# Convolution taps in PSUM, gate products on GpSimd: one change to the up-projections of a two-layer trunk

## The chip, the core and the metric

The kernel runs on one core of a Trainium2 chip. The core has five engines: TensorE (PE) multiplies matrices and writes its sums to PSUM, VectorE (DVE) and ScalarE (ACT) work on elements and reach both SBUF and PSUM, GpSimd (POOL) works on elements in SBUF, and SyncE (SP) issues DMA transfers. The metric is the device time of one execution in microseconds (us); lower is better.

## What is computed

The reference is a trunk of two decoder layers in fp32, with 512 tokens and a model width of 1024. Each layer has a mixer, a gated MLP with a short convolution, and an embedding that is gated in. The change lies in the MLP:

```
D_MODEL, SEQ, D_FF, FFN_CONV_K = 1024, 512, 2816, 3

def _conv_ffn(h, w_up, conv_w, conv_b, w_down):
    u = _causal_depthwise_conv(h @ w_up, conv_w) + conv_b
    gate, up = jnp.split(u, 2, axis=-1)
    return (jax.nn.gelu(gate, approximate=False) * up) @ w_down

for i in range(2):
    x = x + mixer_i(rms_norm(x, mix_norm[i]))
    x = x + _conv_ffn(rms_norm(x, ffn_norm[i]), w_up[i], conv_w[i], conv_b[i], w_down[i])
    x = x + sigmoid(rms_norm(x, ple_norm[i]) @ ple_w_gate[i]) * (p[i] @ ple_w_proj[i])
```

The convolution runs over tokens: each of the 5632 columns of `h @ w_up` is multiplied by its own three weights at lags 0, 1 and 2, and added up with a bias. The RMS factor of each token, called `R` below, is not applied to `h`; the kernel multiplies the projected columns by it, ahead of the taps.

## The kernel before

**Layout.** Activations stand with features on the 128 partitions and the 512 tokens along the free axis. A projected column block is thus a tile of 128 x 512, one PSUM bank.

**Precision.** Every fp32 product is made of three faster ones: both operands are split into a high and a low part, and `mm3` (lines 165 to 171) issues high x high, high x low, low x high. Weights arrive by DMA as `raw` tiles and are split on the chip: ScalarE rounds to the high part `wh` (line 149, or line 825 in `cut_blocks`) and VectorE subtracts to get the low part `wl` (lines 150 and 826). TensorE's third product waits for `wl`.

**Groups.** The up-projection works in 11 groups per layer. A group has four column blocks: two of the value half, made by `value` with `mm3`, and two of the gate half. The gate blocks are computed by a scheme with seven products of half-size blocks instead of eight (`seven`, products at lines 878 to 880), for which VectorE forms differences of weight blocks: two in `first_forms` (lines 849 and 850) and two in `more_forms` (line 857, whose result is cut as `t2`, and line 860, whose result enters the cut called `last` in `seven`). The gate blocks come out in the PSUM banks X and Y, the value blocks in V1 and in a bank that was begun ahead of the group (the late column). Y lacks one term, which is copied to SBUF as `more` and added by VectorE at line 930. All of a group's products are matmuls of 128 x 128 by 128 x 256: 180 of them.

**After the products.** `taps` handles one column block: VectorE multiplies by `R` into an SBUF tile `z` (line 927; for Y it adds `more` at line 930 and multiplies at line 934), ScalarE multiplies `z` by the lag-0 weight and adds the bias, into one half of a tile pair `zt` (line 935), and VectorE adds the two lagged terms (line 937, on 511 and 510 tokens). A group has two such pairs, `g` for the gate and `y` for the value, from a ring of two buffers; `z` comes from a ring of three. `close` then applies Gelu to `g` on ScalarE (line 1087), and `place` multiplies gate and value on VectorE: two products of 128 x 512 for the first four groups of a layer (line 992), one of 128 x 1024 for the others (line 1002). From the fifth group on, `split_one` cuts the product of four groups earlier for the down-projection (lines 108 and 109).

**Order.** TensorE's order is written by hand (`manual_schedule`); each group issues the late column of the next group between its own V1 and its last products. VectorE, ScalarE, GpSimd and the SP queue get their order from a scheduler in the program's builder, with a few written constraints (`issue_after`). An engine runs its instructions in that order, and waits on semaphores for what other engines make.

**Elsewhere.** The pair buffers are used again in the down-projection, where weights are loaded straight into them (`load_inner`), and in layer 1 as halves for its last steps (`half`). There, in `ple1`, the output tiles come from the `z` ring (`result`, line 1423), and one more tile is kept in it.

Of the kernel before, what the change touches and what calls it, by code (L numbers as in the profile page):

```python
# [10 lines left out]
F32 = mybir.dt.float32  # L11
# [3 lines left out]
AF = mybir.ActivationFunctionType  # L15
ALU = mybir.AluOpType
# [3 lines left out]
P = 128  # L20
S = 512
# [42 lines left out]
class Kernel:  # L64
# [763 lines left out]
        n = 2 if wide else 1  # L828
        return lambda j, c: (h[:, n * j + c, :], l[:, n * j + c, :])

    def seven_forms(self, ev, od, raw=None):


        plain = self.first_forms(ev, od, raw)
        return plain, self.cut_blocks(ev), self.more_forms(ev, od)

    def first_forms(self, ev, od, raw=None):

# [11 lines left out]
        nc.vector.tensor_tensor(b12, b22, b12, ALU.subtract)  # L850
        return plain

    def more_forms(self, ev, od):

        nc = self.nc
        b11, b21, b22 = ev[:, :, :P], od[:, :, :P], od[:, :, P:]
        nc.vector.tensor_tensor(b11, b22, b11, ALU.subtract)
        with self.tc.high_priority(offset=40):
            t2 = self.cut_blocks(b11, False)
        nc.vector.tensor_tensor(b21, b21, b11, ALU.subtract)  # L860
        return t2

    def seven(self, od, ws, xg, forms, keep=True):
# [43 lines left out]
    def ffn(self, i, project, next_gain):  # L907


        nc, a, tc = self.nc, self.a, self.tc  # L910
        gain = self.g_ffn[i]
        wu = a["ffn_w_up"][i].rearrange("(k p) n -> p k n", p=P)
        w0, w1, w2, bb = self.fcv

        mine, other = (("a0", "a1"), ("b0", "b1"))[:: 1 - 2 * i]
        with tc.tile_pool(name=f"ffn{i}", bufs=1) as fp:
            self.mlp = fp
            kept, acts, fours = [None] * NF, [None] * NF, []
            groups = NF // 2

            def both():
                return fp.tile([P, 2, S], F32, tag="zt", name=self.nm("zt"), bufs=2)

            def taps(y, ps, f, more=None, behind=None):
                z = fp.tile([P, S], F32, tag="z", name=self.nm("z"), bufs=3)
                if more is None:
                    nc.vector.tensor_tensor(z, ps, R, ALU.mult)  # L927
                else:
                    h2 = lambda x: x.rearrange("p (u t) -> p u t", u=2)
                    nc.vector.tensor_tensor(  # L930
                        h2(z), h2(ps), more.unsqueeze(1).to_broadcast([P, 2, S // 2]), ALU.add
                    )
                    with tc.issue_after(behind.ins) if behind else nullcontext():
                        nc.vector.tensor_tensor(z, z, R, ALU.mult)
                nc.scalar.activation(y, z, AF.Identity, scale=w2[:, f : f + 1], bias=bb[:, f : f + 1])  # L935
                for tap, w in ((1, w1), (2, w0)):
                    nc.vector.scalar_tensor_tensor(  # L937
                        out=y[:, tap:], in0=z[:, : S - tap], scalar=w[:, f : f + 1], in1=y[:, tap:],
                        op0=ALU.mult, op1=ALU.add,
                    )  # L940

# [22 lines left out]
            def prepare(d, behind=None):  # L964

                if d == 0:
                    values.append(load_values(-1))
                rv = values.pop()
                with tc.issue_after(behind.ins) if behind else nullcontext():
                    w0 = column(rv, rv.shape[2] // P - 1)  # L970
                rg = self.raw(ND, 256)
                nc.sync.dma_start(rg, wu[:, :, 256 * d : 256 * d + 256])
                ev, od = self.by_parity(rg)
                ws = self.seven_forms(ev, od, rg)
                values.append(load_values(d))
                return self.seven(od, ws, xg, self.forms), w0, column(values[0], 0)

# [8 lines left out]
            def place(d, g, y):  # L986

                f = 2 * d
                if f < 8:
                    kept[f : f + 2] = [self.fp.tile([P, S], F32, tag=other[0], name=self.nm("u")) for _ in range(2)]  # L990
                    for u in range(2):
                        nc.vector.tensor_tensor(kept[f + u], g[:, u], y[:, u], ALU.mult)
                    return
                if d == groups - 1:
                    x = y
                else:
                    if f % 4 == 0:
                        fours.append(self.four(fp, F32))
                    x = fours[-1][:, f % 4 : f % 4 + 2]
                kept[f : f + 2] = [x[:, 0], x[:, 1]]  # L1000
                pairs[f] = x
                nc.vector.tensor_tensor(x, g, y, ALU.mult)

            pairs = {}

# [49 lines left out]
            with tc.manual_schedule(engines={ET.PE}):  # L1055
                late = begin(0, steps, w0c)
                close = lambda: None
                for d in range(groups):
                    g, y = both(), both()
# [9 lines left out]
                    if d == 0:  # L1069
                        R = self.spread()  # L1070
                    X, Y, more = next(steps)
# [280 lines left out]
    def ple1(self, fp):  # L1352
# [3 lines left out]
        nc, a, tc = self.nc, self.a, self.tc  # L1356
# [63 lines left out]
                self.mm3(pj, sl(pT[k], t), (w[0][:, k, :], w[1][:, k, :]), start=k == 0, stop=k == 1)  # L1420
            return pj

        def result():
            return fp.tile([P, S], F32, tag="z", name=self.nm("so"), bufs=3)

        def keep(banks, tag):
            out = []
# [33 lines left out]
        with tc.manual_schedule(engines={ET.PE, ET.DVE, ET.Activation}):  # L1461
            add(X, "e1", w11, first=True)
            wt1.append(chunk(b11[:, 2:, :]))
            minus(b11, b22, b11)
            steps = [(j, i, both, Q[i]) for j in range(J) for i in range(2)]
            add(None, "s1", wt1, first=True, order=steps[:2])

            sq = self.by_token()
            ka = [self.sp.tile([P, S], F32, tag=g, name=self.nm("keep"), bufs=n) for g, n in (("acc", 1), ("sq", 2))]
            for k, x in zip(ka, X):  # L1470
                nc.scalar.copy(k, x)
            wt2 = chunks(b11)
            pT = self.load_p(1, fp, pin)
            sums = self.few(NT, "ss")
            for t in range(NT):
                junk = self.sp.tile([P, P], F32, tag="vrow", name=self.nm("junk"))
                nc.scalar.activation(junk, sq[:, t * P : (t + 1) * P], AF.Copy, accum_out=sums[:, t : t + 1])
            self.end_norm(sums)
            add(None, "s1", wt1, order=steps[2:])
            minus(b12, b22, b12)  # L1480
            kd = keep(Q, "R")
            wt3 = chunks(b12)
            wj = chunk(wj_raw[:, 2:, :])
            steps = [(j, i, both, X[i]) for j in range(J) for i in range(2)]
            add(None, "s2", wt2, order=steps[:4])
            xs = [back(1, t) for t in (2, 3)]
            add(None, "s2", wt2, order=steps[4:])
            kb = [self.sp.tile([P, S], F32, tag="sq", name=self.nm("keep"), bufs=2), result()]
            for k, x in zip(kb, X):
                nc.scalar.copy(k, x)  # L1490
            pjs = [proj(t, wj) for t in (2, 3)]
            w22 = chunks(b22)
            minus(b11, b21, b11)
            wt4 = [chunk(b11[:, :2, :])]
            nc.scalar.activation(self.few(NT, "rs", 4), self.r, AF.Sigmoid)
            add(X, "s3", wt3)
            ss = [summed(X[t], kd[t]) for t in (0, 1)]
            for t in (0, 1):
                finish(1, t + 2, ss[t], xs[t], pjs[t], ss[t])
            steps = [(j, i, both, Q[i]) for j in range(J) for i in range(2)]  # L1500
            add(None, "s4", w22, order=steps[:6])
            xs = [back(1, t) for t in (0, 1)]
            pjs = [proj(t, wj) for t in (0, 1)]
            wt4.append(chunk(b11[:, 2:, :]))
            wj = chunk(wj_raw[:, :2, :])
            add(None, "s4", w22, order=steps[6:])
            ss = [summed(Q[t], kb[t]) for t in (0, 1)]

            halves = ((0, H // 2), (H // 2, H))
            Y = [Q[0]] + [y[:, : H // 2] for y in (Q[1], X[0])]  # L1510
            for t in (0, 1):
                finish(1, t, ss[t], xs[t], pjs[t], ss[t])
            nc.scalar.copy(Y[0], ka[0])
            nc.scalar.copy(Y[1], ka[1][:, : H // 2])
            steps = [(j, i, both, X[i]) for j in range(J) for i in range(2)]
            add(None, "o2", wt4, order=steps[:6])
            xs = [back(0, t) for t in (2, 3)]
            pjs = [proj(t, wj) for t in (2, 3)]
            w21 = chunks(b21)
            add(None, "o2", wt4, order=steps[6:])  # L1520
            for t in (0, 1):
                finish(0, t + 2, X[t], xs[t], pjs[t])
                if t == 0:
                    nc.scalar.copy(Y[2], ka[1][:, H // 2 :])
            add(None, "o1", w21, order=[(j, 0, both, Y[0]) for j in range(J)])
            xs = [back(0, t) for t in (0, 1)]
            pjs = [proj(t, wj) for t in (0, 1)]
            finish(0, 0, Y[0], xs[0], pjs[0])
            for y, c in zip(Y[1:], halves):
                add(None, "o1", w21, order=[(j, 1, c, y) for j in range(J)])  # L1530
                finish(0, 1, y, xs[1], pjs[1], None, *c)
# [471 lines left out]
```

## Time and profile before

| what | value |
|---|---|
| time of three runs | 1201.72, 1200.26 and 1200.0 us; median 1200.26 |
| span of the profiled execution | 1199.4 us (the median is 0.86 above it) |
| TensorE busy | 1192.4 us, 99% |
| VectorE busy | 966.4 us, 81% |
| ScalarE busy | 671.1 us, 56% |
| GpSimd busy | 44.8 us, 4% |
| nine groups of the up-projection, layer 0 and layer 1 | 184.00 and 184.51 us |

A row of a timeline has the start and the duration in us, the engine, the line of the kernel, the operation, the tile that is written and those that are read, partitions x elements, and a count. In brackets stands how long the engine had been idle, and which instruction ended that. A row of a source line has minimum, median and maximum duration in ns. A row of the view by windows has, for each engine, busy time and number of instructions in the stretch. Start-to-start distances are a little shorter than durations, because an engine's instructions overlap at their ends.

### The profile page before, as it was taken

Reading aid. Unit: us, or ns where it says so; the run is one execution under the profiler, and the core shown is the slowest. Engines: PE = TensorE matmul, PEld = TensorE weight load, DVE = VectorE, ACT = ScalarE, POOL = GpSimd, SP = SyncE. Lnnn points to the kernel's source line nnn. Section 1 sums busy time; section 2 is a strip of 40 time slices with the busy share of each in tenths; the row PEclk is TensorE's granted clock in tenths of the full one; section 3 lists DMA queues with packets and bytes.
Section 4 is the critical chain, followed back from the end, with each engine's and each line's share of the span. In section 5 each row is a group of like instructions: output and inputs, shape, how many; then the busy total and the mean of one; then the engine's idle time right before and its main releaser. Section 6 shows DMA issues by size and latency. Waiting matters only on the chain.

```text
span 1199.4 us, 19840 instructions
## 1 busy us (share of the span) xinstructions
PE 1192.4 (99%) x8074; PEld 1076.9 (90%) x8074; DVE 966.4 (81%) x1543; ACT 671.1 (56%) x1093; POOL 44.8 (4%) x64
## 2 busy tenths in 40 slices
PE   9999999999999999999999999999999999999998
PEld 8877789999999989888988988899999999888887
DVE  6786687898999986746679876687989999988595
ACT  7466565655565753534563655555555656655374
POOL 2610000000000000000100000000000000000000
PEclk9999999999999999999999999999999999999999
DMA  7232222333332342232322222223233333322601
GB/s 223 72 97 80 74 88 71 106 106 106 106 107 89 113 138 84 87 106 86 107 93 70 75 68 70 88 72 115 97 112 100 106 106 114 124 89 98 210 1 71
DMA packets 113216, 117.74 MB, mean 98 GB/s; under 512 B 2873, under 2 KB 108403, under 8 KB 113125
## 3 DMA queue, kind: packets, MB, share of 16 engines
q1 hardware_dynamic: 111760, 115.35, 29.5%
q8 instruction: 63, 1.03, 0.4%
q0 software_dynamic: 560, 0.42, 0.3%
q10 hardware_dynamic: 804, 0.70, 0.2%
q14 instruction: 29, 0.23, 0.1%
HBM read 114.37 MB, written 2.10 MB: 97 GB/s over the span
## 4 chain that ended last, share of the span: by engine, by line
PE 92%; DVE 5%; ACT 1%; DMA 1%; issue 0%; ACTq 0%; DVEq 0%
PE ps L169 14%; PE ps L170 14%; PE ps L171 14%; PE pa L170 7%; PE pa L171 7%; PE pa L169 7%; PE ps L878 5%; PE ps L880 5%; PE ps L879 5%; PE pa L878 2%; PE pa L880 2%; PE pa L879 2%; PE ps L1400 1%; PE ps L1398 1%; PE ps L1399 1%; DVE wl L150 1%
## 5 line engine op out<-in xcount | busy, mean ns | idle before, releaser
L149 ACT ACTIVATE wh<-raw 128x1024 fp32r<-128x1024 f32 (+4 forms) x154 | 152.5, 992 | 128.9 <-PE ps L170 92.8
L150 DVE TENSOR_TENSOR wl<-raw,wh 128x1024 fp32r<-128x1024 f32 (+4 forms) x154 | 175.3, 1140 | 57.9 <-ACT wh L149 57.0
L825 ACT ACTIVATE wh<-raw 128x1024 fp32r<-128x1024 f32 x78 | 83.0, 1064 | 115.8 <-DVE raw L850 75.9
L937 DVE SCALAR_TENSOR_TENSOR zt<-z,vfa,zt 128x510 f32<-128x510 f32 (+1 forms) x176 | 131.0, 745 | 0.3
L826 DVE TENSOR_TENSOR wl<-raw,wh 128x1024 fp32r<-128x1024 f32 x78 | 95.4, 1222 | 12.8 <-ACT wh L825 12.8
L171 PE MATMUL pa<-b,wl 128*128 128x256 f32 x352 | 97.3, 276 | 0.1
L171 PE MATMUL pa<-a,wl 128*128 128x256 f32 x352 | 97.2, 276 | 0.0
L169 PE MATMUL pa<-b,wh 128*128 128x256 f32 x352 | 97.2, 276 | 0.0
L169 PE MATMUL pa<-a,wh 128*128 128x256 f32 x352 | 97.2, 276 | 0.0
L170 PE MATMUL pa<-b,wh 128*128 128x256 f32 x352 | 97.2, 276 | 0.0
L170 PE MATMUL pa<-a,wh 128*128 128x256 f32 x352 | 97.2, 276 | 0.0
L935 ACT ACTIVATE zt<-z,vfb 128x512 f32<-128x512 f32 x88 | 71.5, 813 | 19.6 <-DVE z L927 9.5
L169 PE MATMUL ps<-b,wh 128*128 128x512 f32 x192 | 76.6, 399 | 0.0
L170 PE MATMUL ps<-b,wh 128*128 128x512 f32 x192 | 75.1, 391 | 0.0
L171 PE MATMUL ps<-b,wl 128*128 128x512 f32 x192 | 75.0, 391 | 0.0
L171 PEld LDWEIGHTS pa<-b,wl 128*128 128x128 f32 x352 | 66.1, 188 | 0.3 <-DVE wl L150 0.3
L169 PEld LDWEIGHTS pa<-b,wh 128*128 128x128 f32 x352 | 66.1, 188 | 0.0
L170 PEld LDWEIGHTS pa<-a,wh 128*128 128x128 f32 x352 | 66.1, 188 | 0.0
L169 PEld LDWEIGHTS pa<-a,wh 128*128 128x128 f32 x352 | 66.1, 188 | 0.0
L170 PEld LDWEIGHTS pa<-b,wh 128*128 128x128 f32 x352 | 66.1, 188 | 0.0
L171 PEld LDWEIGHTS pa<-a,wl 128*128 128x128 f32 x352 | 66.1, 188 | 0.0
L878 PE MATMUL ps<-four,wh 128*128 128x256 f32 x232 | 64.7, 279 | 0.0
(472 smaller groups left out, 3667.7 us busy)
## 6 DMA issues: line engine op xcount, KB each, us to landing
raw<-in_ffn_w_up_dram SPq DMA_DIRECT2D x42, 1024.0 KB, 5.1
raw<-in_ffn_w_down_dram SPq DMA_DIRECT2D x13, 1024.0 KB, 4.8
raw<-in_hy_w_in_dram SPq DMA_DIRECT2D x8, 1024.0 KB, 5.0
raw<-in_gla_w_in_dram SPq DMA_DIRECT2D x8, 1024.0 KB, 5.1
raw<-in_ffn_w_down_dram SPq DMA_DIRECT2D x8, 768.0 KB, 4.1
raw<-in_ple_w_gate_dram SPq DMA_DIRECT2D x6, 1024.0 KB, 4.6
raw<-in_hy_w_out_dram SPq DMA_DIRECT2D x16, 256.0 KB, 3.9
raw<-in_gla_w_out_dram SPq DMA_DIRECT2D x4, 1024.0 KB, 4.7
```

Of the source, the lines that this page charges most:

```text
L149: nc.scalar.activation(hv, v, AF.Copy)
L150: self.rest_cut = nc.vector.tensor_tensor(lv, v, hv.bitcast(F32), ALU.subtract)
L169: mm(out, lh, rh, start=start, stop=False, **kw)
L170: mm(out, lh, rl, start=False, stop=False, **kw)
L171: mm(out, ll, rh, start=False, stop=stop, **kw)
L825: nc.scalar.activation(h, src, AF.Copy)
L826: nc.vector.tensor_tensor(l, src, h.bitcast(F32), ALU.subtract)
L878: mm(out, wh, xh, start=first and j == 0, stop=False, **kw)
L879: mm(out, wh, xl, start=False, stop=False, **kw)
L880: mm(out, wl, xh, start=False, stop=j == ND // 2 - 1, **kw)
L935: nc.scalar.activation(y, z, AF.Identity, scale=w2[:, f : f + 1], bias=bb[:, f : f + 1])
L937: nc.vector.scalar_tensor_tensor(out=y[:, tap:], in0=z[:, : S - tap], scalar=w[:, f : f + 1], in1=y[:, tap:], op0=ALU.mult, op1=ALU.add,)
```

## The change

`taps` no longer has the tile `z`. VectorE multiplies by `R` in place, in the PSUM bank (for Y, it first adds `more` in place); ScalarE and the two lagged additions read that bank. Of the differences of weight blocks, the last one (`b21`) is made by GpSimd in the up-projections; `place` multiplies gate and value on GpSimd. The ring of pairs has three buffers instead of two. In `ple1` the output tiles come from the pairs, and the `z` ring has one buffer left, for the tile that is kept. The memory of both rings together is the same, 14 KB per partition.

```
-    def more_forms(self, ev, od):
+    def more_forms(self, ev, od, last=None):
...
-        nc.vector.tensor_tensor(b21, b21, b11, ALU.subtract)
+        (last or nc.vector).tensor_tensor(b21, b21, b11, ALU.subtract)
...
-                return fp.tile([P, 2, S], F32, tag="zt", name=self.nm("zt"), bufs=2)
+                return fp.tile([P, 2, S], F32, tag="zt", name=self.nm("zt"), bufs=3)

             def taps(y, ps, f, more=None, behind=None):
-                z = fp.tile([P, S], F32, tag="z", name=self.nm("z"), bufs=3)
-                if more is None:
-                    nc.vector.tensor_tensor(z, ps, R, ALU.mult)
-                else:
+                if more is not None:
                     h2 = lambda x: x.rearrange("p (u t) -> p u t", u=2)
                     nc.vector.tensor_tensor(
-                        h2(z), h2(ps), more.unsqueeze(1).to_broadcast([P, 2, S // 2]), ALU.add
+                        h2(ps), h2(ps), more.unsqueeze(1).to_broadcast([P, 2, S // 2]), ALU.add
                     )
-                    with tc.issue_after(behind.ins) if behind else nullcontext():
-                        nc.vector.tensor_tensor(z, z, R, ALU.mult)
-                nc.scalar.activation(y, z, AF.Identity, scale=w2[:, f : f + 1], bias=bb[:, f : f + 1])
+                with tc.issue_after(behind.ins) if behind else nullcontext():
+                    nc.vector.tensor_tensor(ps, ps, R, ALU.mult)
+                nc.scalar.activation(y, ps, AF.Identity, scale=w2[:, f : f + 1], bias=bb[:, f : f + 1])
                 for tap, w in ((1, w1), (2, w0)):
                     nc.vector.scalar_tensor_tensor(
-                        out=y[:, tap:], in0=z[:, : S - tap], scalar=w[:, f : f + 1], in1=y[:, tap:],
+                        out=y[:, tap:], in0=ps[:, : S - tap], scalar=w[:, f : f + 1], in1=y[:, tap:],
...
-                ws = self.seven_forms(ev, od, rg)
+                ws = self.seven_forms(ev, od, rg, nc.gpsimd)
...
-                        nc.vector.tensor_tensor(kept[f + u], g[:, u], y[:, u], ALU.mult)
+                        nc.gpsimd.tensor_tensor(kept[f + u], g[:, u], y[:, u], ALU.mult)
...
-                nc.vector.tensor_tensor(x, g, y, ALU.mult)
+                nc.gpsimd.tensor_tensor(x, g, y, ALU.mult)
...
-        def result():
-            return fp.tile([P, S], F32, tag="z", name=self.nm("so"), bufs=3)
+        result = self.half
...
-            kb = [self.sp.tile([P, S], F32, tag="sq", name=self.nm("keep"), bufs=2), result()]
+            kb = [
+                self.sp.tile([P, S], F32, tag="sq", name=self.nm("keep"), bufs=2),
+                fp.tile([P, S], F32, tag="z", name=self.nm("keep"), bufs=1),
+            ]
```

More of the change, by code (lines that the diff above doesn't have):

```diff
@@ L829, in cut_blocks, with seven_forms @@
         return lambda j, c: (h[:, n * j + c, :], l[:, n * j + c, :])
-    def seven_forms(self, ev, od, raw=None):
+    def seven_forms(self, ev, od, raw=None, last=None):
         plain = self.first_forms(ev, od, raw)
-        return plain, self.cut_blocks(ev), self.more_forms(ev, od)
+        return plain, self.cut_blocks(ev), self.more_forms(ev, od, last)
     def first_forms(self, ev, od, raw=None):
```

## The prediction

> **What bounds the kernel now.** I read the page of the profile first: engine totals and the chain that ended last.
>
> ```profile
> span 1199.4 us, 19840 instructions
> ...
> PE 1192.4 (99%) x8074; PEld 1076.9 (90%) x8074; DVE 966.4 (81%) x1543; ACT 671.1 (56%) x1093; POOL 44.8 (4%) x64
> ...
> PE 92%; DVE 5%; ACT 1%; DMA 1%; issue 0%; ACTq 0%; DVEq 0%
> ```
>
> TensorE sets the end: 99% busy, 92% of the chain. VectorE has 81% and 5% of the chain, so the change, which takes work off VectorE only, can win only where TensorE stands still for it. The view by windows, over nine groups of the up-projection in each layer:
>
> ```profile
> core 0: us, PE busy (x) PEld busy (x) DVE busy (x) ACT busy (x) POOL busy (x), PEclk, DMA share, GB/s
> 206.94:390.94 184.00, 184.00 (x1623) 183.90 (x1621) 170.08 (x228) 107.77 (x151) 0.00 (x0) 1.00 0.31 101
> 824.34:1008.85 184.51, 184.43 (x1622) 184.00 (x1621) 170.23 (x228) 107.41 (x151) 0.00 (x0) 1.00 0.31 101
> ```
>
> The granted clock is 1.00, and a group has 180 matmuls. Their pitch stands in TensorE's timeline.
>
> ```profile
> 302.76 0.28 PE L171 MATMUL pa<-a,wl 128*128 128x256 f32 x1
> ...
> 312.28 0.28 PE L880 MATMUL ps<-four,t 128*128 128x256 f32 x1
> ...
> 313.64 0.28 PE L171 MATMUL pa<-a,wl 128*128 128x256 f32 x1
> ```
>
> From 312.28 to 313.64 are twelve matmuls, 0.1133 us each. Nine groups without a stall are 9 x 180 x 0.1133 = 183.6 us: the first window loses 0.40, the second 0.91, together **1.31 us**. That is all that a faster VectorE can give back in these stages; the first group of each layer and the down-projections lie outside.
>
> How near is VectorE to being late? Its timeline, and ScalarE's beside it:
>
> ```profile
> 292.92 1.22 DVE L826 TENSOR_TENSOR wl<-raw,wh 128x1024 fp32r<-128x1024 f32 x1
> ...
> 297.27 1.23 DVE L1002 TENSOR_TENSOR four<-zt,zt 128x1024 f32<-128x1024 f32 x1 [1.19 <-ACT zt L1087]
> 298.72 1.23 DVE L150 TENSOR_TENSOR wl<-raw,wh 128x1024 fp32r<-128x1024 f32 x1 [0.22 <-ACT wh L149]
> ...
> 309.78 0.68 DVE L860 TENSOR_TENSOR raw<-raw 128x512 f32<-128x512 f32 x1
> 310.38 0.68 DVE L826 TENSOR_TENSOR t<-raw,t 128x512 fp32r<-128x512 f32 x1
> 310.98 0.68 DVE L927 TENSOR_TENSOR z<-pa,R 128x512 f32<-128x512 f32 x1
> 311.58 1.21 DVE L150 TENSOR_TENSOR wl<-raw,wh 128x1024 fp32r<-128x1024 f32 x1
> ```
>
> ```profile
> 291.79 1.07 ACT L825 ACTIVATE wh<-raw 128x1024 fp32r<-128x1024 f32 x1 [0.92 <-PE ps L879]
> ...
> 296.18 1.06 ACT L1087 ACTIVATE zt<-zt 128x1024 f32<-128x1024 f32 x1 [1.48 <-DVE zt L937]
> 297.35 0.36 ACT L902 COPY ps<-ps 128x256 f32<-128x256 f32 x1
> 297.62 1.06 ACT L149 ACTIVATE wh<-raw 128x1024 fp32r<-128x1024 f32 x1
> ```
>
> Low parts of weights reach TensorE with these leads: for V1, 311.58 + 1.21 = 312.79 against 313.64, **0.85 us**; for t2, 311.06 against 312.28, 1.22; for the late value column, 299.95 against 302.76, 2.81. VectorE's loop is tied to TensorE once per group: the cut of 292.92 starts when ScalarE's cut, released by TensorE, ends (291.79 + 1.07 = 292.86). VectorE then runs with two pauses, 1.19 for the Gelu and 0.22 for L149, until the next such cut. Any delay that it can't make good there is carried into the next group.
>
> **The change, part by part.** The built program keeps TensorE's order. VectorE loses 52 instructions, which GpSimd gains: 22 of L860 and 30 of the products at L992 and L1002.
>
> *L860 to GpSimd.* VectorE's chain between 298.72 and the V1 cut gets shorter by its pitch, 310.38 - 309.78 = **0.60 us**. Its result goes to the "last" cut, much later. On GpSimd it runs beside a tap and the addition, both with an operand in PSUM.
>
> *Gate times value to GpSimd.* VectorE no longer waits 1.19 for the Gelu nor multiplies (1.23). But its next operation, L150, still waits for ScalarE's L149, which ends at 297.62 + 1.06 = 298.68, so the cut of the late column starts no earlier; of this part nothing shortens the loop. Behind it, the split four groups later and the down-projection read the products; those are far off. The SP queue's loads into the pair buffers wait for the last product, but they are issued a down-projection stage ahead.
>
> What it can cost: GpSimd's product starts at the Gelu's end, 297.24, and runs through 298.72. GpSimd and VectorE beside each other, at the only place of this trace where both run:
>
> ```profile
> L518 POOL TENSOR_TENSOR m<-q,ropeS x8: 726/830/1182, 44.2 to 55.6; 128x256 f32<-128x256 f32 x8
> ```
>
> ```profile
> 44.24 3.26 POOL L518 TENSOR_TENSOR m<-q,ropeS 128x256 f32<-128x256 f32 x4 [9.21 <-ACT q L557]
> ...
> 49.58 1.04 POOL L738 TENSOR_TENSOR R<-R 128x512 f32<-128x512 f32 x1
> ...
> 54.88 1.62 POOL L518 TENSOR_TENSOR m<-q,ropeS 128x256 f32<-128x256 f32 x2 [0.39 <-DVE m L521]
> ```
>
> ```profile
> 45.67 1.25 DVE L516 TENSOR_TENSOR m<-q,ropeC 128x512 f32<-128x512 f32 x1
> ...
> 54.06 0.68 DVE L521 TENSOR_TENSOR m<-m,m 128x512 f32<-128x512 f32 x1
> ...
> 56.78 0.68 DVE L516 TENSOR_TENSOR m<-q,ropeC 128x512 f32<-128x512 f32 x1
> ```
>
> The same L516, two inputs in SBUF, takes 1.25 beside GpSimd and 0.68 without it: one waits for the other. L150 has two inputs in SBUF too, so I let it wait until the product is done. The hand-over to GpSimd is 54.88 - (54.06 + 0.68) = 0.14. No row shows 128x1024 on GpSimd. Call its time p. Low end: 1.04 and two more of the step from 256 to 512 elements, 1.04 + 2 x (1.04 - 0.726) = 1.67. High end: four of 0.726, 2.90. Twice the 512 row, the nearest, is 2.08. L150 is then late by 297.24 + 0.14 + p - 298.72 = p - 1.34; the 0.60 from L860 pays for that, so the loop keeps its pace up to **p = 1.94**. Above it the excess e = p - 1.94 is carried from group to group, and TensorE is late once ten groups of it pass the 0.85 lead: 10e - 0.85 per layer. At 1.67 the cost is 0; at 2.08, 2 x (1.4 - 0.85) = 1.1 us. I take the middle between these, **+0.5**, since even a small recovery of the blocked operation would bring 2.08 to 0; the ends are 0 and, at 2.90, 2 x (9.6 - 0.85) = 17.5.
>
> The Trainium skill, "GPSIMD Engine Reference", section 3.1 Elementwise, measures 4497 ns for 2048 fp32 elements in a tensor_tensor. An estimate from that page for half as many is 2.25 us; by it e would be 0.31 and the cost 2 x (3.1 - 0.85) = 4.5 us. No run here shows it.
>
> *Taps in PSUM.* Durations with the operand in PSUM and in SBUF, by source line:
>
> ```profile
> L112 DVE SCALAR_TENSOR_TENSOR a<-ps,vec,a x8: 741/744/752, 7.1 to 17.3; 128x512 fp32r<-128x512 f32 x8
> L112 DVE SCALAR_TENSOR_TENSOR a<-xT,vec,a x8: 745/747/750, 495.0 to 523.2; 128x512 fp32r<-128x512 f32 x8
> ```
>
> Reading PSUM is free (744 against 747 ns), so the eight taps of a group cost what they did. New is VectorE's writing to PSUM: four products with R and one addition per group. No row has it; ScalarE's copy within PSUM (L902, 0.36 for 256 columns) isn't slow. I take 0. Low end 0; as the high end I take 0.25 each, somewhat under half of the 1.25 - 0.68 = 0.57 by which L516 stretched when it shared its inputs: 1.25 a group, against the 0.60. A column's bank is held until its last tap instead of its first product. There are four of each kind, taken in turn, and the tap ends microseconds before the slot's next matmul: 0, hidden by the rotation; without that cover TensorE would wait for a tap, 0.74 a time.
>
> The Trainium skill, "VectorE: DVE Perf Modes", section "The TRN2 errata", charges 120 fixed cycles for a PSUM source and 58 for SBUF, some 65 ns more by its clock. The trace disagrees: 744 against 747 ns. If it held here, eight taps would add 0.52 a group.
>
> *Three pair buffers, one z buffer.* Same memory. The third pair lets the next taps start while GpSimd still reads the last one; without it the products would hold the loop. In the last step of layer 1 the halves come from pairs whose output transfers landed long before: 0.
>
> *What comes back.* Of the 1.31 I give half, **-0.65**: the 0.60 raises V1's lead to 1.45, but single stalls may be other waits.
>
> Sum: 1199.4 - 0.65 + 0.5 + 0 = 1199.25 us of span. The median of the runs shown, 1200.26, is 0.86 above that span, so I forecast **1200.1 us**: no change. About 0.2% (2.4 us) is what a measurement of this kernel can tell from none.
>
> **The rivals.**
>
> *R1, slower: GpSimd's product holds VectorE.* For it: L516 above, at 1.25; GpSimd's rows spread up to 1182 ns for 256 elements, so its own work stretches as well. The Trainium skill speaks for it too: "SBUF — State Buffer", section "Who interferes with whom", has a VectorE instruction with two SBUF inputs contend with a GpSimd one that reads SBUF, as an exclusive lock; the trace agrees, 1.25 against 0.68. Against it: 1.94 is near the middle of my p, and the taps, with one operand now in PSUM, may slip past. At p = 2.4: 2 x (4.6 - 0.85) = 7.5, or 1199.4 - 0 + 7.5 + 0.86 = 1207.8; at 2.90, 1217.8. It decides from p = 2.1 or so.
>
> *R2, slower: VectorE's in-place writes to PSUM are dear.* From 0.12 each (five fill the 0.60) it costs: at 0.25, 0.65 a group, 2 x (6.5 - 0.85) = 11.3, or 1211.6. Only the missing row speaks for it.
>
> *R3, faster: VectorE had been behind every stall.* The 1.31 goes whole, and I allow as much again for the first groups and the down-projections, which have short stalls too: 1199.4 - 2.62 + 0.86 = 1197.6. Against it: those stalls are short and scattered, and 1197.6 is only at the edge of what can be told.
>
> *R4, the change moves nothing on the path.* It ends at 1200.3 and belongs to "same".
>
> **How the numbers follow.** No change (my forecast and R4) 0.51, R1 0.33, R2 0.07, R3 0.09. Faster 0.09, same 0.51, slower 0.40. The low end is R3's 1197.6; the high end takes in R1 to p = 2.6 (2 x (6.6 - 0.85) = 11.5) and R2's 1211.6: 1211.8. The likeliest case's own range is 1198.5 to 1202.
>
> **What would show it.** L860 and the products appear in GpSimd's rows at about 1.0 and 2.1 us. VectorE's busy time in each window falls by about 9 x 1.8 us, and the Gelu's wait is gone from it. L150 after the Gelu starts 0.3 to 0.7 later, the V1 cut no later than before. The in-place products stay at 0.68. TensorE's window stays at 183.6 to 184.5. I am wrong if L150's mean rises by more than 0.6 and TensorE waits for `wl`, or if the in-place rows grow by 0.1.

## The result, and the profile after

The changed kernel takes 1213.63 us (median of 4 runs, 1211.58 to 1215.12) against 1200.96 us: a ratio of 1.0103, with a 95% interval of 1.0088 to 1.0117. It is slower by 12.7 us. The forecast was 1200.1, and its range ended at 1211.8.

The page of the changed kernel, the same rows as before:

```profile
span 1213.3 us, 19946 instructions
...
PE 1200.5 (99%) x8074; PEld 1080.8 (89%) x8074; DVE 951.2 (78%) x1491; ACT 666.8 (55%) x1093; POOL 153.3 (13%) x116
...
PE 64%; DVE 23%; ACT 4%; issue 3%; DMA 3%; POOL 2%; ACTq 0%; SPq 0%; POOLq 0%; DVEq 0%
```

VectorE is less busy, as it should be (951 instead of 966 us), and yet its share of the chain rose from 5% to 23%. To see where the time went, I cut both traces at the same matmuls of TensorE's order, which the change leaves alone. The stretches are the nine groups of layer 0, its last group with the down-projection, and the same for layer 1. The changed kernel's view by windows (columns as before):

```profile
core 0: us, PE busy (x) PEld busy (x) DVE busy (x) ACT busy (x) POOL busy (x), PEclk, DMA share, GB/s
207.19:392.25 185.06, 184.86 (x1623) 184.11 (x1621) 160.25 (x204) 105.08 (x149) 34.80 (x22) 1.00 0.31 100
392.25:547.48 155.23, 152.69 (x888) 132.62 (x887) 113.79 (x153) 76.46 (x111) 17.64 (x4) 0.99 0.31 102
832.01:1016.70 184.69, 184.55 (x1623) 183.99 (x1621) 160.03 (x204) 105.24 (x149) 34.79 (x22) 1.00 0.31 101
1016.70:1158.83 142.13, 139.31 (x782) 120.40 (x781) 112.19 (x157) 74.41 (x109) 16.61 (x3) 0.99 0.37 123
```

The same stretches of the kernel before are 184.00, 149.07, 184.51 and 136.11 us long. So 1.1 and 0.2 us were lost in the groups, and **6.2 and 6.0 us behind them**, where the prediction had priced nothing. (These are single profiled executions. The one of the changed kernel was the slowest of its four, 1215.12 us.) The chain of waits of the changed kernel says what stands there:

```profile
419.21 12.91 POOL zt L999
...
432.14 0.37 SPq L1157
...
432.61 8.29 DMA raw<-in_ffn_w_down_dram
```

The last group's product of gate and value (line 999 now) occupies GpSimd for 12.91 us. The SP queue then issues a load into a pair buffer (line 1157), which had waited for that product, and behind it the next weights. In the kernel before, too, a load into a pair buffer waited for the product, which ended at 417.29 + 1.22 = 418.51 on VectorE, and the same weights followed:

```profile
417.29 1.22 DVE L1002 TENSOR_TENSOR zt<-zt,zt 128x1024 f32<-128x1024 f32 x1
```

```profile
418.63 0.37 SPq L1160 DMA_DIRECT2D zt<-in_ffn_w_down_dram  x1
424.99 0.37 SPq L1151 DMA_DIRECT2D raw<-in_ffn_w_down_dram  x1
```

In the changed kernel:

```profile
419.64 0.37 SPq L1148 DMA_DIRECT2D raw<-in_ffn_w_down_dram  x1
432.14 0.37 SPq L1157 DMA_DIRECT2D zt<-in_ffn_w_down_dram  x1
432.61 3.72 SPq L1148 DMA_DIRECT2D raw<-in_ffn_w_down_dram  x2
```

The load of weights at 424.99 moved to 432.61. TensorE then waits for it, and what follows the wait is slow as well:

```profile
444.41:447.82 3.41, 3.41 (x11) 2.75 (x10) 3.34 (x8) 1.75 (x3) 0.00 (x0) 0.50 0.00 0
1072.46:1075.88 3.42, 3.42 (x18) 3.37 (x17) 2.90 (x5) 0.63 (x1) 0.00 (x0) 0.50 0.03 5
```

The granted clock (third number from the end: the share of full speed that TensorE was given) was 0.50 for 3.4 us behind the wait in each layer; in the kernel before it is 1.00 through both down-projections. At most half of 3.41 is lost by it, so I estimate up to 1.7 us per layer out of the 6.2 and 6.0. Not every execution has this: the mean granted clock was 0.997, 0.998 and 0.997 in those of 1215.12, 1212.84 and 1214.43 us, and 1.000 in the shortest, of 1211.58. Of the other traces, only the one with line 860 back on VectorE has such a stretch, in layer 0 alone.

What VectorE did during the last group's product, at its beginning and at its end:

```profile
418.66 0.95 DVE L150 TENSOR_TENSOR wl<-raw,wh 128x768 fp32r<-128x768 f32 x1
419.53 1.22 DVE L109 TENSOR_TENSOR four<-four,four 128x1024 fp32r<-128x1024 f32 x1
...
429.76 0.70 DVE L1206 TENSOR_TENSOR xT<-xT,ps 128x512 f32<-128x512 f32 x1
430.36 2.04 DVE L1028 TENSOR_TENSOR four<-four 128x256 f32<-128x256 f32 x1
```

From 418.66 to 429.76 VectorE ran without a pause, and each operation took two operands from SBUF. None of them was stretched, so GpSimd was the one that waited. Line 1206 reads one operand from PSUM; the operation behind it took 2.04 us where line 1028 takes 0.42 elsewhere, and the product ended at 432.12. Less the 2.41 us that the product takes in the groups (below), that is 429.71: GpSimd got in where line 1206 starts. Layer 1 shows the same.

In the groups the blocking goes the other way. VectorE and GpSimd in one of them:

```profile
310.37 0.69 DVE L927 TENSOR_TENSOR ps<-ps,more 128x512 f32<-128x512 f32 x1
310.97 0.90 DVE L826 TENSOR_TENSOR t<-raw,t 128x512 fp32r<-128x512 f32 x1
...
319.71 2.27 DVE L150 TENSOR_TENSOR wl<-raw,wh 128x1024 fp32r<-128x1024 f32 x1 [2.45 <-ACT wh L149]
```

```profile
310.02 1.30 POOL L860 TENSOR_TENSOR raw<-raw 128x512 f32<-128x512 f32 x1 [9.90 <-DVE raw L857]
318.49 2.41 POOL L999 TENSOR_TENSOR four<-zt,zt 128x1024 f32<-128x1024 f32 x1 [7.17 <-ACT zt L1084]
```

The product takes p = 2.41 us, and L150, which starts inside it, 2.27 instead of 1.22. Line 927, with an operand in PSUM, runs beside GpSimd at 0.69 as if alone. That L150 ends 1.08 us behind the product (321.98 against 320.90): it waited for the whole product and then ran.

### The profile page after: what moved, and what is told of

It is laid out like the page before. It is cut to its first block, busy times and chain, and to the rows that moved or that the text cites. A ratio compares the mean times of both kernels' runs of the same rounds, so it can differ in the third digit from the quotient of the medians.

```text
span 1213.3 us, 19946 instructions
## 1 busy us (share of the span) xinstructions
PE 1200.5 (99%) x8074; PEld 1080.8 (89%) x8074; DVE 951.2 (78%) x1491; ACT 666.8 (55%) x1093; POOL 153.3 (13%) x116
## 4 chain that ended last, share of the span: by engine, by line
PE 64%; DVE 23%; ACT 4%; issue 3%; DMA 3%; POOL 2%; ACTq 0%; SPq 0%; POOLq 0%; DVEq 0%
PE ps L169 11%; PE ps L171 11%; PE ps L170 11%; DVE zt L934 6%; DVE wl L826 4%; DVE wl L150 3%; PE pa L170 3%; PE pa L171 3%; PE pa L169 3%; PE ps L878 3%; PE ps L880 3%; PE ps L879 3%; POOL zt L999 2%; DMA raw<-in_ffn_w_down_dram 2%; DVE ps L931 1%
## 5 line engine op out<-in xcount | busy, mean ns | idle before, releaser
L150 DVE TENSOR_TENSOR wl<-raw,wh 128x1024 fp32r<-128x1024 f32 (+4 forms) x154 | 188.1, 1222 | 104.2 <-ACT wh L149 103.6
L860 POOL TENSOR_TENSOR raw<-raw 128x512 f32<-128x512 f32 x22 | 29.2, 1327 | 304.3 <-DVE raw L857 304.3
L934 DVE SCALAR_TENSOR_TENSOR zt<-ps,vfa,zt 128x511 f32<-128x511 f32 x88 | 65.3, 742 | 0.2
```

The source lines that it names most:

```text
L150: self.rest_cut = nc.vector.tensor_tensor(lv, v, hv.bitcast(F32), ALU.subtract)
L860: (last or nc.vector).tensor_tensor(b21, b21, b11, ALU.subtract)
L934: nc.vector.scalar_tensor_tensor(out=y[:, tap:], in0=ps[:, : S - tap], scalar=w[:, f : f + 1], in1=y[:, tap:], op0=ALU.mult, op1=ALU.add,)
```

## The experiments

Theory A: the last group's product is starved (kept waiting) by VectorE, the SP queue stands still for it, and that is most of the loss; the rest is the product's blocking of L150 in the groups (the prediction's R1). The rivals were B, by which the loop of the groups or VectorE's writes to PSUM (R2) are all of it, and C, by which the changed buffers leave the loads less room, whatever the product takes.

**The last product back on VectorE.**

```
-                nc.gpsimd.tensor_tensor(x, g, y, ALU.mult)
+                (nc.vector if d == groups - 1 else nc.gpsimd).tensor_tensor(x, g, y, ALU.mult)
```

> The last group's product of each layer goes back to VectorE, everything else stays as changed. Theory A (that product waits 12.9 us on GpSimd behind VectorE's unbroken run of operations with two SBUF inputs, and the SP queue's next loads stand behind it, which is where 11 of the 14 us are lost): about 1202.5 us, 1201.5 to 1204, and the two stalls of the down-projections (5.5 us each) are gone while the 3 us of the up-projections stay. Theory B (the loss is in the loop of the groups, or in VectorE's writing to PSUM): 1212 to 1214. Theory C (less room for the loads, whatever the product takes): 1212 to 1214.

Measured: 1205.39 us (1204.85 to 1206.96), ratio to before 1.0042 (1.0029 to 1.0054). One product per layer is worth **8.2 us**. That is well past what B or C allow, but 1.4 us above the end of A's own range: the stretches behind the groups fell to 150.82 and 137.59, still 1.75 and 1.5 above before. VectorE comes out of the groups late: the cut of `t` in the down-projection starts at 445.32, against 442.30 where all products are on VectorE (below), and only 1.1 us of that are TensorE's own delay in the groups. The granted clock is 1.000 in this trace, so the tail at half the clock is part of the 8.2 us.

**The SP queue freed, the product left where it is.**

```
-                nc.sync.dma_start(t, wd[:, k0 + q : k1 : 2, cols(u)])
+                (nc.gpsimd if q else nc.sync).dma_start(t, wd[:, k0 + q : k1 : 2, cols(u)])
```

> The second of the two loads into pair buffers of each inner block is issued from GpSimd's queue, behind the product, so the loads in the SP queue behind it don't wait for the product any more; the product itself stays starved (12.9 us). Theory A (the price is the SP queue standing still): 8 to 11 us come back, 1203 to 1206. If the price is the product's lateness itself (its split for the down-projection, or VectorE's operations that were blocked), nothing or little comes back: 1211 to 1214.

Measured: 1206.80 us (1206.43 to 1207.16), ratio 1.0050 (1.0036 to 1.0063). GpSimd's timeline still has the long product, with the load behind it:

```profile
418.77 12.90 POOL L999 TENSOR_TENSOR zt<-zt,zt 128x1024 f32<-128x1024 f32 x1 [15.19 <-ACT zt L1084]
431.97 0.85 POOL L1157 DMA_DIRECT2D zt<-in_ffn_w_down_dram  x1 [0.30 <-POOL zt L999]
```

The product is as late as before, the next weights are issued at 427.74 instead of 432.61, and 6.8 of the 8.2 us are gone. Most of the price is therefore what stands behind the product in the SP queue, not the product; the other 1.4 us weren't traced. The granted clock is 1.000 here, too.

**An operation added to VectorE.** Right ahead of the product of the last group:

```
+                if d == groups - 1:
+                    nc.vector.tensor_reduce(self.few(1, "gap"), g[:, 0], mybir.AxisListType.X, ALU.max)
```

> Work is added to VectorE: a reduction over one 128x512 tile, which has one input only, right after the Gelu of the last group of each layer (its result isn't used). The product stays on GpSimd. Theory A says that GpSimd gets in when VectorE does something that doesn't take two SBUF inputs: the product then takes 2 to 3.5 us instead of 12.9, and the time is about 1203 us (1201.5 to 1205), though VectorE does 1.4 us more. If the product is slow by itself (it is the only one whose output lies in a pair buffer and over one of its inputs), it still takes 12.9 and the time is 1213 to 1215.

Measured: 1214.60 us (1214.29 to 1215.29), ratio 1.0116 (1.0102 to 1.0130): no gain at all, though the product took 2.68 us. The stretches behind the groups fell to 151.90 and 138.58, but the nine groups of a layer rose to 187.92 in both layers. Nothing waits there; TensorE's own rows are further apart:

```profile
293.81 0.28 PE L878 MATMUL ps<-four,t 128*128 128x256 f32 x1
293.93 0.28 PE L879 MATMUL ps<-four,t 128*128 128x256 f32 x1
294.05 0.28 PE L880 MATMUL ps<-four,t 128*128 128x256 f32 x1
```

These start 0.12 us apart instead of 0.113, and so do about four in ten of the stretch's 1620 matmuls; the others stay at 0.113. The reduction's result had got a new small tile, two buffers of 32 bytes per partition, which can shift what is allocated after it. So the run was repeated with the result in a tile that exists already (`self.few(NT, "ss")[:, :1]`):

> As the run with the added reduction, but its result goes into a small tile that exists already, so that no other tile's address in SBUF moves (in the first one a new tile of 2 x 32 bytes per partition was added, and TensorE's distance between matmuls of the up-projection rose from 113.8 to up to 119.5 ns without any wait). Theory A with the address as the spoiler: the product takes 2 to 3 us, the distances are 113.8 again, and the time is near that of the last product on VectorE, 1205.4 us: 1204 to 1207. If the reduction itself slows TensorE or the down-projection, it stays at 1213 to 1215.

Measured: 1207.35 us (1206.80 to 1207.94), ratio 1.0052 (1.0040 to 1.0065), with 184.65 and 185.51 us for the nine groups. The two runs differ in that tile alone, so it was the spoiler. The product and VectorE around it:

```profile
418.20 2.68 POOL L1001 TENSOR_TENSOR zt<-zt,zt 128x1024 f32<-128x1024 f32 x1 [15.19 <-ACT zt L1086]
```

```profile
418.54 0.67 DVE L1000 TENSOR_REDUCE ss<-zt 128x1 f32<-128x512 f32 x1
419.13 2.82 DVE L109 TENSOR_TENSOR four<-four,four 128x1024 fp32r<-128x1024 f32 x1
```

With one more operation on VectorE, the kernel is 6.3 us faster than without it. The product isn't slow by itself.

**What lets GpSimd in?** Two more runs with a short operation at that place, one with one input (`tensor_reduce` over `g[:, 0, :8]`), one with two (`tensor_tensor` of `g[:, 0, :8]` and `g[:, 1, :8]`), both into the existing tile:

> As the run with the added reduction, but over 8 columns only: a short VectorE operation with one input in SBUF, after the Gelu of the last group. If GpSimd needs only one such operation between two with two SBUF inputs, however short, the product takes 2 to 3.5 us again and the time is 1205 to 1208. If it needs some length (the reduction of 512 columns took 0.67 us), it still takes about 12.9 and the time is 1212 to 1215.

> The control: at the same place, an operation as short, but with two inputs in SBUF; the order of VectorE's other instructions is the same as in the run with the short reduction. By theory A it doesn't let GpSimd in: 12.9 us for the product and 1212 to 1215 us. If the boundary of any added instruction, or the wait for the Gelu before it, or the moved order of a few later instructions is what helps, the product takes 2 to 3.5 us here too: 1205 to 1208.

Measured: 1207.06 us (1206.66 to 1207.92) with one input, and 1207.92 us (1207.44 to 1208.86) with two; ratios 1.0050 (1.0037 to 1.0064) and 1.0055 (1.0040 to 1.0071). The control did what theory A said that it would not. In its trace the product starts during L150, and the added operation waits for it:

```profile
418.92 2.69 POOL L1001 TENSOR_TENSOR zt<-zt,zt 128x1024 f32<-128x1024 f32 x1 [15.20 <-ACT zt L1086]
```

```profile
418.39 0.94 DVE L150 TENSOR_TENSOR wl<-raw,wh 128x768 fp32r<-128x768 f32 x1
419.26 2.37 DVE L1000 TENSOR_TENSOR ss<-zt 128x8 f32<-128x8 f32 x1
```

So an operation with one operand in SBUF isn't needed. All added operations have in common that they need the Gelu's result, which also releases the product. One more thing differs in the traces. In the changed kernel VectorE's queue took up a wait for the line 150 that starts at 420.67 already at 416.0, before the Gelu began. In the last three runs the same wait stands at 418.1 to 418.8, when the Gelu had just ended: the added operation had held the queue back. Whether that, the dependence, the boundary itself or something else opens the door stays open.

**Line 860 back on VectorE**, products on GpSimd (`self.seven_forms(ev, od, rg)` without `nc.gpsimd`):

> Line 860 goes back to VectorE in the up-projections; the gate products stay on GpSimd. By the loop (each group, VectorE's cut is blocked about 1.05 us by GpSimd's product and the 0.60 us of line 860 pays part of it) the excess per group grows from 0.4 to about 1.0 us: 20 groups, about 12 us more, 1225 us (1219 to 1229). If it is line 860 on GpSimd that delays the cut of t2 (0.90 instead of 0.69 us) and that costs the 3 us of the up-projections, the time falls instead, to 1210 to 1212.

Measured: 1220.54 us (1218.46 to 1221.69), ratio 1.0163 (1.0149 to 1.0177): 6.9 us slower than the changed kernel, inside the range given by the loop, but little more than half of the 12 us expected. The nine groups take 186.27 and 186.39 us in the profiled execution, the fastest of its four. Moving line 860 to GpSimd helps.

**All products on VectorE**, line 860 on GpSimd, taps in PSUM, three pairs (`nc.vector` in both places of `place`), and then **line 860 on VectorE as well**, so that nothing is left on GpSimd:

> All gate products on VectorE again; line 860 stays on GpSimd, the taps in PSUM, three pair buffers. If what is left over the kernel before in the run with only the last product moved back (1205.4 against 1200.75) is the products' blocking of the cut in the groups, about 2 us in the two up-projections go: 1202 to 1204. If line 860 on GpSimd or the taps in PSUM is the cause, it stays at 1205 to 1206.

> Nothing on GpSimd: only the taps in PSUM, three pair buffers and the tiles of the last step of layer 1. If VectorE's writing to PSUM costs nothing (0.68 to 0.69 us, as in the changed kernel's rows) and the rest of the loss was GpSimd's: 1199 to 1202. If the banks are held too long, or the taps in PSUM cost VectorE or ScalarE time: 1204 or more.

Measured: 1199.16 us (1198.60 to 1200.24), ratio **0.9984** (0.9975 to 0.9993), with line 860 on GpSimd; 1200.79 us (1199.63 to 1202.05), ratio 1.0000 (0.9991 to 1.0009), with nothing on it. The first is faster than both kernels, if by 0.16% only. Its view by windows, nine groups of each layer:

```profile
core 0: us, PE busy (x) PEld busy (x) DVE busy (x) ACT busy (x) POOL busy (x), PEclk, DMA share, GB/s
207.06:390.66 183.60, 183.60 (x1622) 183.60 (x1621) 166.02 (x218) 106.20 (x150) 10.47 (x9) 1.00 0.31 101
...
824.37:1007.97 183.60, 183.60 (x1623) 183.60 (x1622) 166.58 (x219) 107.00 (x151) 11.02 (x10) 1.00 0.31 101
```

183.60 is the time of 9 x 180 matmuls without a stall: all of the 1.31 us came back, and the time is below the 1202 to 1204 that I had expected. With nothing on GpSimd the nine groups already take 183.60 and 184.39, so 0.52 of the 1.31 us need no GpSimd.

**Products in halves on GpSimd**, the last one on VectorE:

```
+                if d == groups - 1:
+                    nc.vector.tensor_tensor(x, g, y, ALU.mult)
+                else:
+                    for u in range(2):
+                        nc.gpsimd.tensor_tensor(x[:, u], g[:, u], y[:, u], ALU.mult)
```

> The last group's product on VectorE; the others on GpSimd, but each as two of 128x512 where it was one of 128x1024, so that VectorE's cut waits for one half (1.30 us) instead of the whole (2.41). If the blocking by the product is what the up-projections lose, L150 after the Gelu takes less than 2.27 us and about 1 to 2 us come back against 1205.4: 1203 to 1204.5. If VectorE is blocked for both halves in a row, the time is the same or worse: 1205 to 1208.

Measured: 1201.11 us (1200.33 to 1203.75), ratio 1.0001 (0.9992 to 1.0010): 4.3 us came back, more than expected, and not in the way expected. L150 isn't shortened to one half; from the fifth group on it alternates. In one group it is blocked by the second half, in the next it gets in between the halves and the second half waits. GpSimd's halves in two groups in a row, and L150 in the same two:

```profile
316.95 2.55 POOL L1003 TENSOR_TENSOR four<-zt,zt 128x512 f32<-128x512 f32 x2 [7.61 <-ACT zt L1088]
...
337.87 3.60 POOL L1003 TENSOR_TENSOR four<-zt,zt 128x512 f32<-128x512 f32 x2 [7.17 <-ACT zt L1088]
```

```profile
318.39 2.19 DVE L150 TENSOR_TENSOR wl<-raw,wh 128x1024 fp32r<-128x1024 f32 x1 [2.67 <-ACT wh L149]
...
339.08 1.23 DVE L150 TENSOR_TENSOR wl<-raw,wh 128x1024 fp32r<-128x1024 f32 x1 [2.45 <-ACT wh L149]
```

**GpSimd's part in the kernel before**, with taps through SBUF and two pairs: line 860 alone, and line 860 with all products.

> The kernel before with line 860 alone on GpSimd: taps through SBUF, two pair buffers, gate products on VectorE. All gate products on VectorE, with taps in PSUM and three pairs, gave 1199.16 against 1200.94 (ratio 0.9984). If the 1.8 us come from VectorE's chain being 0.60 shorter, they come here too: 1198.6 to 1199.8. If the taps in PSUM are needed for it (beside GpSimd's line 860, VectorE's operations with one operand in PSUM aren't blocked, those in SBUF are): 1200 to 1202.

> Line 860 and all gate products on GpSimd, in the kernel before: taps through SBUF, two pair buffers. It tells what the taps in PSUM and the third pair spare. With the tap products and additions reading two SBUF operands, VectorE's unbroken run is longer and the product in the groups is starved too, and with two pairs the next taps wait for it: slower than the changed kernel by far, 1225 to 1290. If taps in PSUM and the third pair have no part in it: 1211 to 1216.

Measured: 1205.99 us (1205.12 to 1206.48), ratio 1.0039 (1.0027 to 1.0052), and 1233.08 us (1231.39 to 1235.73), ratio 1.0268 (1.0254 to 1.0282). Line 860 on GpSimd, which gains 1.6 us with taps in PSUM, loses 4.8 in the kernel before; I had allowed 1202 at most. VectorE and GpSimd in the first of the two:

```profile
310.57 0.74 DVE L937 SCALAR_TENSOR_TENSOR zt<-z,vfa,zt 128x510 f32<-128x510 f32 x1
311.36 1.67 DVE L826 TENSOR_TENSOR t<-raw,t 128x512 fp32r<-128x512 f32 x1
```

```profile
310.89 1.59 POOL L860 TENSOR_TENSOR raw<-raw 128x512 f32<-128x512 f32 x1 [19.13 <-DVE raw L857]
```

Between line 857 and the cut of `t` there is one tap, which takes two operands from SBUF here. GpSimd starts behind it, and the cut waits: 1.67 us instead of 0.68. In the changed kernel a tap and the addition stand there, both with an operand in PSUM, and the cut takes 0.90. In the second run, 197.91 and 196.92 us for the nine groups, the cut of `t` (1.67) and L150 (2.28) are both blocked in each group from the fifth on; in the first four, ScalarE waits 18.5 us in 8 waits for a pair buffer that a product still reads, since there are only two. The product itself takes 2.41 there as well: contrary to what I had expected, it isn't starved in the groups.

In this order, the change comes apart as follows, by medians. From the changed kernel's 1213.63, the last product back on VectorE gives 8.2, the others 6.2 more; line 860 back costs 1.6, and the taps with the pair buffers make 0.15 of difference. That is 1200.94 again, by construction; in another order the shares differ, as line 860 shows, which is worth 6.9 us with the products on GpSimd and 1.6 without.

## Why the prediction was wrong

The forecast was no change. The rival R1 had the mechanism for nearly half of the loss, and one step, priced at nothing, hid the rest.

- *The step that failed:* "The SP queue's loads into the pair buffers wait for the last product, but they are issued a down-projection stage ahead." The load was seen, and the wait, but I looked at the duration that the product has in the groups, and not at what VectorE does beside the last one. There VectorE is never idle, the product took 12.91 us, and the queue it holds carries the next weights, too: they were issued at 432.61 instead of 424.99, and TensorE waited for them. That step is worth 8.2 us, as the run with this one product moved shows, and 6.8 of them are the SP queue, as the run on the other queue shows. Up to 3.4 us of the loss, by the estimate above, are TensorE's half clock behind the waits, for which the prediction has no term.
- *The size of p:* the range was 1.67 to 2.90, and I worked near its low end, between 1.67 and 2.08. Measured: 2.41. By the step's own formula, e = 2.41 - 1.94 = 0.47 and 2 x (4.7 - 0.85) = 7.7 us; the products of the other groups cost 6.2. R1 at p = 2.4 stated 7.5. So the blocking and the carrying over from group to group were right, and the choice of p was wrong. The row of 128x512 that it was worked out from, L738 at 1.04, multiplies a tile by itself; line 860, with two tiles of that size, took 1.30. Whether that is the reason wasn't tried. R1 had it against itself that 1.94 is near the middle of p; in 1.67 to 2.90 it lies in the lowest quarter.
- That the formula's 7.7 comes near 6.2 is in part luck. L150 is blocked in seven of the groups of a layer (five at about 2.27 us, two at 1.8 to 1.9), not ten, since in the first groups the product comes in two parts. In layer 0 the cut for V1 starts 2.41, 2.79 and 3.17 us behind its group's first matmul, 0.38 more each time instead of 0.47, and then TensorE's groups take 20.7 to 20.8 us instead of 20.4. So with only the last product moved back, the nine groups of the two layers (184.71 and 185.05 us) lose 2.6 us against the run with all products on VectorE; 3.3 more are lost behind them, which the formula doesn't have.
- The Trainium skill, "GPSIMD Engine Reference", section 3.1 Elementwise, by which I had estimated 2.25 us, was nearer to 2.41 than the 2.08 from my rows.
- *Line 860:* right. I gave it half of 1.31; in the windows (one execution each) it brings 0.79, and the taps in PSUM with the third pair the other 0.52. The condition that I named in passing, operands in PSUM beside it, decides: in the kernel before, without it, 4.8 us are lost.
- *Taps in PSUM:* right. The in-place products take what they took (0.684 to 0.686 us before, by median), by source line:

```profile
L931 DVE TENSOR_TENSOR ps<-ps,R x44: 679/687/697, 206.3 to 1037.4; 128x512 f32<-128x512 f32 x44
```

R2 is out, and the run with nothing on GpSimd is at 1.0000.
- The Trainium skill, "SBUF — State Buffer", section "Who interferes with whom": the trace agrees that VectorE with two SBUF inputs and GpSimd block each other (2.27 against 1.22), and that VectorE with one input in PSUM is spared (0.69).
- *What I had said would show it:* TensorE waiting for `wl` came true. L150 rose by 0.6 to 1.05 in the groups where it was blocked; its mean over the whole program rose by 0.08 only (from 1.140 to 1.222 us). The sign that was missing from the list is GpSimd's longest single row.

## What to carry to other kernels

Work moved to an idle GpSimd isn't free: in these traces it and VectorE wait for each other where VectorE takes two operands from SBUF. Find out what VectorE does during each instance of it, the last one ahead of a new stage above all, and let operands of VectorE's neighbours come from PSUM. Before pricing a wait at nothing, follow the queue behind it: a single late buffer held up loads that had nothing to do with it, and behind the wait TensorE ran at half its clock for a while. In this kernel one small operation on GpSimd beside PSUM operands gained 0.16%; the larger products added to it cost 14 us.

## What the runs showed of the hardware

- GpSimd's product of 128x1024 took 2.41 us in the groups and 12.91 us beside a run of VectorE operations with two SBUF operands and no pause. By the rows above, one waits for the other's whole instruction, and VectorE, going from one instruction to the next, kept its turn for more than 10 us.
- One added operation of 8 columns on VectorE, with one SBUF input or two, ended that: 2.7 us for the product. Why, isn't settled.
- A new tile of 64 bytes per partition raised the distance of about four in ten matmuls from 0.113 to about 0.12 us and the nine groups from 184.65 and 185.51 to 187.92 us; the run that used an existing tile differs in that alone. That addresses are the reason, and which tile's, wasn't tried.
- Behind the two waits of the changed kernel, TensorE's granted clock was 0.50 for 3.41 us each, and matmuls of 128x512 started 0.43 us apart (445.08, 445.51) instead of 0.23 (439.41, 439.64).
